# Another order of the head stages in the second super-block of a hybrid decoder step on one core

## The chip, the cores and the metric

One core of one Trainium2 chip runs the whole kernel. The metric is device time in microseconds: the median of the runs of one program on the chip. Lower is better.

## What the kernel computes

A prompt of 16 + 2048 tokens and 8 sample tokens pass through a trunk of two layers. Each layer projects the tokens (1024 wide) to 5120 channels, sends them through three groups of heads, gates each by SiLU, projects the 1536 mixed channels back and normalises. The core of the reference:

```python
u = jnp.einsum('btd,de->bte', x, w_in).astype(f32)
rg_c, rg_buf_new = _causal_conv(rg_in, rg_buf, rg_conv_w)
rg_h, h_new = _rglru(rg_c + rg_conv_b, h0, ...)                    # A: RG-LRU
y_rg = rg_h * jax.nn.silu(rg_z)
...
o, s_ret_new = _chunk_run(_ret_step, RET_CHUNK, s_ret, (q, k, v), lead)      # B: retention
...
o, s_gdn_new = _chunk_run(_gdn_step, GDN_CHUNK, s_gdn, (gq, gk, gv, g_log, beta), lead)   # C: gated DeltaNet
...
mix = jnp.concatenate([y_rg, y_ret, y_gdn], -1)
out = jnp.einsum('bte,ed->btd', mix, w_out.astype(f32))
y = _layernorm(DEEPNORM_ALPHA * x + out, ln_w, ln_b)
```

Inside a chunk of 64 tokens the gated DeltaNet solves a triangular system; the kernel inverts these triangles explicitly. The heads of one group don't depend on each other, nor the groups on one another, except that every DeltaNet head needs all key stages and the inverses.

## The kernel before

The tokens of a layer are taken in two super-blocks: columns 0 to 1023 (two blocks of 512), then 1024 to 2071 (three blocks of 384, 384 and 280, the samples among them). In each, the work is a row of sixteen **stages**, written out in the table `STAGES` (line 29): K0 to K3 make the DeltaNet keys, A0 to A3 are slabs of RG-LRU, B0 to B3 retention heads, C0 to C3 DeltaNet heads. A stage has slabs of 128 output channels: one for K, two for A (the convolution and the gate), four for B (q, k, v, gate), three for C. A slab is a projection `proj` (line 466 ff.): 24 matmuls for every token block, named `pj<-arena`, because float32 is computed as three products of two rounded halves; the weights are staged in `raw`, split on ScalarE and GpSimd and kept in `arena`. Two PSUM banks hold `pj`.

What a head does behind its projections (its recurrence and norm: `retention_bg`, `delta_bg`, `rglru_gates` and `rglru_scan`) is a generator that the `Pump` interleaves with the projections of the **next** stage. The triangular inverses (`inverses`, names `as_`, `tt`, `t`, `tn`, `prod`) are a second such stream. It begins behind the key stages, is spread over the slabs up to C0 (`n_inv` counts them) and is finished, in the order of writing, before C0.

`Recorder` notes all instructions in this order and then issues them in another: a list scheduler, driven by assumed costs, takes on every engine the earliest noted instruction that it expects to be ready (one that reads PSUM goes ahead on VectorE and ScalarE). So `STAGES` sets a priority, and the scheduler an order on every engine. On the chip each engine then keeps to that order.

Tiles share places, and a new tile waits for the last user of the old one. Those that matter here:

- `g` (the gate, two places): a stage's gate waits for the output of the stage two before it, to the end of the DMA `mix_d<-g` that stores it.
- `q` (two places): holds the q of a B or C stage; the inverses borrow one for their matrices `as_`. In the second super-block that place goes on to the q of C0.
- `a1` to `a4` (one place each): the working tiles of the generator that is running: `kv`, `sn` (B), `kk`, `uv`, `wq` (C), `r`, `ix`, `ch`, `cl`, then `s`, `y` (A). So the generators of successive stages follow each other.
- `kT` (two places): k of B, C and K, the convolution's result `c` of A; at the end of a layer two of the three places in which the weights of the output projection are staged (`raw<-in_wout`).

In the last stage of the second super-block (`end` in `rglru`) `c` lies in `tab`, and the gates' generator is started inside the stage. From there `wo_load` and `wo_free` bring the output weights in twelve pieces (`wh`, `wl` for the first two, `arena` for the others), as the projections' input is given up. Then the output projection runs over 17 row tiles (`pj` and `po`/`pd` of 512 columns).

```python
rows of the loop over stages (sblock):
n_inv = sum(len(SLABS[st[0]]) for st in STAGES[sb][4:STAGES[sb].index("C0")])
if i_st == 4:
    pump.drain()
    scales()
    pump.add_aux(inverses(), (78 if samp else 60) / (n_inv * nmm))
```

Of the kernel before, what the change touches and what calls it, by code (L numbers as in the profile page):

```python
# [25 lines left out]
SCK = 128.0 ** -0.5  # L26
HALF = 1024

STAGES = ("K0 K1 K2 K3 A0 B0 A1 C0 C1 B1 A2 C2 C3 B2 A3 B3".split(), "K0 K1 K2 K3 A0 B0 A1 C0 B1 C1 B2 C2 B3 C3 A2 A3".split())
NEG = -32768.0  # L30


# [306 lines left out]
def hymba_step(ctx: ExitStack, tc: tile.TileContext, x0t, x0, win, wab, wout, wg, vec, fbc, const, rope,  # L339
# [64 lines left out]
    def big(tag, name=None, n=1052, dt=F32, bufs=2):  # L404
        return wk.tile([128, n], dt, tag=tag, name=name or tag, bufs=bufs)
# [4 lines left out]
    def softplus(out, x, P, n, pre):  # L410
# [10 lines left out]
        for d in (15, 13, 11, 9, 7, 5, 3):  # L421
# [8 lines left out]
    SLABS = dict(K=(28,), A=(0, 4), B=(8, 12, 16, 20), C=(24, 32, 36))  # L430
    order = [(l, j + int(st[1])) for l in range(DEPTH) for sb in range(2) for st in STAGES[sb]
             for j in SLABS[st[0]]]
# [117 lines left out]
    def layer(l):  # L550
# [42 lines left out]
        def sblock(sb):  # L593
# [751 lines left out]
            def rglru(i):  # L1345
                end = samp and STAGES[1][-1] == f"A{i}"
                c = big("tab", "c", bufs=1) if end else big("kT", "c")
                conv(i, slab(), [VV("rgcw")[:, 4 * q + i:4 * q + i + 1] for q in range(4)], VV("rgcb")[:, i:i + 1], c)
                wgt = lay.tile([128, 2, 128], F32, name="wgt", tag="wgt", bufs=1)
                SP.dma_start(wgt, wg[l, :, i])  # L1350
                rx = []
                gates = rglru_gates(i, c, wgt, rx), 2 * len(blks) + 7
                if end:
                    pump.add(*gates)
                g = gate(slab())
                if not end:
                    pump_next(*gates)
                pump_next(rglru_scan(i, rx, g), 5)
# [75 lines left out]
            hook["last"] = last_slab  # L1434
            n_inv = sum(len(SLABS[st[0]]) for st in STAGES[sb][4:STAGES[sb].index("C0")])
            for i_st, st in enumerate(STAGES[sb]):
                if st == STAGES[1][-1] and samp:
                    wo_load(l)
# [193 lines left out]
    def wo_load(l):  # L1632
        raws, wo = [], {}
        wos["tiles"] = wo

        def stage(i):
            if i < 12:
                raws.append(big(("kT", "kT", "raw")[i % 3], "raw", n=1024, bufs=(2, 2, 1)[i % 3]))
                SP.dma_start(raws[i], wout[l, WO_ORDER[i]])

        def gen(lo, hi):
            for i in range(lo, hi):
                k = WO_ORDER[i]
                if k < 10:
                    wh, wl = arena[:, 2048 * k:2048 * k + 1024], arena[:, 2048 * k + 1024:2048 * k + 2048]
                else:
                    wh = wk.tile([128, 1024], F32R, tag=("q", "v")[k - 10], name="wh", bufs=2)
                    wl = wk.tile([128, 1024], F32R, tag=("q", "v")[k - 10], name="wl", bufs=2)
                A.copy(wh, raws[i])
                V.tensor_tensor(wl, raws[i], wh.bitcast(F32), op=OP.subtract)  # L1650
                wo[k] = (wh, wl)
                if i == 0:
                    stage(2)
                stage(i + 3)
                yield

        stage(0)
        stage(1)
        wos["gen"] = gen
        pump.add_aux(gen(0, 2), 2 / 60)  # L1660
# [129 lines left out]
```

## Time and profile before

| | us |
|---|---|
| median of 3 runs | 3231.73 (3229.43 to 3248.26) |
| profiled execution | 3247.79 |
| its span, first to last instruction | 3246.0 |
| TensorE busy in the span | 3143.9 |
| VectorE busy | 2040.6 |
| ScalarE busy | 1295.8 |
| GpSimd busy | 683.9 |

The profiled execution took 1.79 us more than its span. It lies near the slowest of the three runs, 16.1 us above their median. A layer takes about half of the span; in the first layer the second super-block runs from about 620 to 1285 us, in the second from about 2235 to 2912 us. PE stands for TensorE's matmuls, DVE for VectorE, ACT for ScalarE, POOL for GpSimd, SP for the queue that issues most DMAs. Every instruction goes through one helper, so all rows show its line 268; an instruction is told by the tile it writes and those it reads. "Idle before" and an engine and tile behind an arrow say how long the engine stood still and whose end it waited for. The granted clock of TensorE is 1.00 at 2.4 GHz and 0.50 at 1.2 GHz.

### The profile page before, as it was taken

The numbers are of one execution on the slowest core, as the hardware profiler recorded it, in microseconds if no ns is written. First come the engines' busy times: TensorE is split into PE (matmuls) and PEld (weight loads), VectorE is DVE, ScalarE is ACT, GpSimd is POOL, SyncE is SP. The second block draws the span as 40 slices with busy tenths as digits, with TensorE's granted clock in tenths as the row PEclk, the third lists the DMA queues.
The fourth block names the chain that finished last, engine by engine and source line by source line (L and its number), as shares of the span: only waits on it lengthen the run. The fifth ranks groups of instructions, "written<-read, shape, count | busy, mean of one in ns | idle before, by whom it ended". The sixth has DMA issues, their size and how long they took to land. (4 is left out here: it accounts for less than half of the span.)

```text
span 3246.0 us, 47389 instructions
## 1 busy us (share of the span) xinstructions
PE 3143.9 (97%) x18876; PEld 2758.9 (85%) x18876; DVE 2040.6 (63%) x3704; ACT 1295.8 (40%) x2732; POOL 683.9 (21%) x651
## 2 busy tenths in 40 slices
PE   8999999998999998999999999999989999998999
PEld 6888888898899998788778888888988999987886
DVE  6876565678745556656478756556876455566554
ACT  4454544543544445211243545444424444453110
POOL 2222221222312221111122222222222122121110
PEclk9999999998999999899999999999978999998999
DMA  4111211321111113555321111122201111135542
GB/s 151 61 67 46 67 49 56 104 82 40 49 46 56 41 51 123 168 167 161 112 95 54 61 47 67 43 67 103 73 33 43 51 58 41 51 108 179 156 143 70
DMA packets 137061, 262.97 MB, mean 81 GB/s; under 512 B 24368, under 2 KB 79600, under 8 KB 136840
## 3 DMA queue, kind: packets, MB, share of 16 engines
q1 hardware_dynamic: 113640, 179.91, 17.7%
q0 software_dynamic: 23200, 80.04, 6.8%
q8 instruction: 148, 2.42, 0.3%
q14 instruction: 73, 0.60, 0.1%
HBM read 195.13 MB, written 65.04 MB: 80 GB/s over the span
## 5 line engine op out<-in xcount | busy, mean ns | idle before, releaser
L268 PE MATMUL pj<-arena 128*128 128x512 f32 (+3 forms) x9760 | 2129.8, 362 | 39.3 <-DVE g L268 24.6
L268 PEld LDWEIGHTS pj<-arena 128*128 128x128 f32 (+1 forms) x9760 | 1637.4, 189 | 198.2 <-DVE g L268 26.5
L268 POOL TENSOR_TENSOR arena<-raw,arena 128x1024 fp32r<-128x1024 f32 x159 | 399.3, 2511 | 1205.2 <-ACT arena L268 1064.0
L268 ACT CAST arena<-raw 128x1024 fp32r<-128x1024 f32 x180 | 188.8, 1049 | 341.1 <-PE pj L268 183.0
L268 DVE SCALAR_TENSOR_TENSOR stg<-stg,eg,pd 128x128 f32<-128x128 f32 x264 | 90.9, 344 | 137.5 <-PE pd L268 135.7
L268 PE MATMUL pj<-arena,ah 128*128 128x512 f32 x512 | 164.8, 403 | 0.9 <-ACT ah L268 0.9
L268 ACT COPY ur<-pj 128x512 f32<-128x512 f32 (+2 forms) x160 | 80.3, 502 | 195.4 <-PE pj L268 194.9
L268 ACT ACT_TABLE_LOAD x106 | 136.0, 1283 | 26.5 <-DMA mix_d<-g 22.0
L268 ACT COPY sw<-pj 64x512 f32<-64x512 f32 (+2 forms) x160 | 80.0, 500 | 107.7 <-PE pj L268 60.4
L268 PEld LDWEIGHTS pj<-arena,ah 128*128 128x128 f32 x512 | 97.7, 192 | 23.8 <-ACT ah L268 1.0
L268 PE MATMUL pj<-arena,al 128*128 128x512 f32 (+1 forms) x296 | 112.3, 400 | 0.1
L268 PEld LDWEIGHTS pz<-stg,wq 128*128 128x128 f32 x512 | 90.2, 189 | 12.7 <-ACT wq L268 3.6
L268 DVE SCALAR_TENSOR_TENSOR g<-g,pj 128x512 f32<-128x512 f32 (+2 forms) x120 | 69.1, 579 | 50.1 <-ACT g L268 49.5
L268 PE MATMUL pz<-stg,wq 128*128 128x128 f32 x512 | 98.8, 274 | 1.6 <-ACT wq L268 1.4
L268 PE MATMUL pd<-kv 128*128 128x128 f32 x512 | 99.2, 276 | 0.0
L268 ACT CAST bh<-mb 128x512 fp32r<-128x512 f32 x32 | 19.8, 619 | 197.9 <-PE po L268 115.6
L268 DVE BATCH_NORM_STATS2 bs<-pz 128x6 f32<-128x128 f32 x128 | 37.9, 296 | 93.6 <-PE pz L268 93.5
L268 ACT ACTIVATE g<-pj 128x512 f32<-128x512 f32 (+2 forms) x120 | 61.5, 514 | 87.4 <-PE pj L268 85.5
L268 PEld LDWEIGHTS pd<-kv 128*128 128x128 f32 x512 | 86.8, 190 | 7.6
L268 PE MATMUL po<-arena,ah 128*128 128x512 f32 x288 | 92.9, 401 | 0.0
L268 ACT ACTIVATE wq<-pz,eg 64x128 f32<-64x128 f32 x128 | 43.0, 360 | 118.8 <-DVE kv L268 74.1
L268 DVE SCALAR_TENSOR_TENSOR qT<-ur,gcw,qT 128x1024 f32<-128x1024 f32 (+1 forms) x48 | 75.8, 1580 | 20.7 <-ACT qT L268 20.4
(388 smaller groups left out, 5166.7 us busy)
## 6 DMA issues: line engine op xcount, KB each, us to landing
raw<-in_win SPq DMA_DIRECT2D x160, 512.0 KB, 3.3
ma<-mix_d SPq DMA_DIRECT2D x31, 512.0 KB, 4.8
mix_d<-g POOLq DMA_DIRECT2D x24, 520.0 KB, 3.0
mix_d<-g POOLq DMA_DIRECT2D x24, 512.0 KB, 3.1
raw<-in_wout SPq DMA_DIRECT2D x24, 512.0 KB, 3.8
xr<-in_x SPq DMA_DIRECT2D x16, 512.0 KB, 4.0
x_d<-yo POOLq DMA_DIRECT2D x16, 512.0 KB, 3.3
sv<-row_d POOLq DMA_DIRECT2D x16, 512.0 KB, 4.4
```

What stands on the lines that cost most here:

```text
L268: return lambda *args, **kw: self._r.note(self._n, op, lambda: f(*args, **kw), args, kw)
```

## The change

One line changes: the sequence of stages of the second super-block, in both layers. The first super-block keeps its own.

```diff
-STAGES = ("K0 K1 K2 K3 A0 B0 A1 C0 C1 B1 A2 C2 C3 B2 A3 B3".split(), "K0 K1 K2 K3 A0 B0 A1 C0 B1 C1 B2 C2 B3 C3 A2 A3".split())
+STAGES = ("K0 K1 K2 K3 A0 B0 A1 C0 C1 B1 A2 C2 C3 B2 A3 B3".split(), "K0 K1 K2 K3 B0 A0 B1 C0 A1 C1 B2 C2 A2 C3 B3 A3".split())
```

The same sixteen stages run, A3 still last. Ahead of C0 there were A0, B0 and A1 with 8 slabs; now there are B0, A0 and B1 with 10, so `n_inv` is 10. Behind each stage its generator runs under another stage: C0 under A1 (before under B1), C2 under A2 (before under B3), C3 under B3 (before under A2), and under the last stage A3 that of B3 (before that of A2).

The instructions on each engine move with it. First VectorE in the second super-block of the first layer, where the scan of A0 ends (`s<-r,hcar,ix`, and `g<-s,g`, which gives A0's gate its output). Before:

```order
L268 SCALAR_TENSOR_TENSOR s<-r,hcar,ix 128x1040
L268 COPY hcar<-s 128x1
L268 TENSOR_TENSOR s<-r,h_121 128x8
L268 TENSOR_TENSOR s<-s,ix 128x8
L268 COPY h_121<-s 128x8
L268 SCALAR_TENSOR_TENSOR g<-s,g 128x1048
L268 SCALAR_TENSOR_TENSOR tt<-as__914,nbs,t_821 128x961
L268 TENSOR_REDUCE t_821<-tt 128x31
L268 STREAM_TRANSPOSE tt<-t_821 128x32x32
L268 SCALAR_TENSOR_TENSOR g<-g,pj 128x384 x2
```

The last row is A1's gate, four rows behind the scan; its tile is the place that A0's `g` gives up. Now, in the same place:

```order
L268 SCALAR_TENSOR_TENSOR s<-r,hcar,ix 128x1040
L268 COPY hcar<-s 128x1
L268 TENSOR_TENSOR s<-r,h_121 128x8
L268 TENSOR_TENSOR s<-s,ix 128x8
L268 COPY h_121<-s 128x8
L268 TENSOR_TENSOR sn<-qk,ct 128x512
L268 SCALAR_TENSOR_TENSOR g<-s,g 128x1048
L268 SCALAR_TENSOR_TENSOR prod<-as__915,nbt,gt 4x100
L268 TENSOR_REDUCE gt<-prod 4x10
L268 TENSOR_TENSOR sn<-qk,ct 128x512
L268 SCALAR_TENSOR_TENSOR prod<-as__915,nbt,gt 4x121
```

The large solve is over by then (only the samples' small one, `prod`, is left), the generator of B1 begins (`sn<-qk`), and the next gate in this place, that of C0, stands 52 rows behind `g<-s,g`.

Second, TensorE in the same super-block, where the third block of C0's first projection waits for the place of `as_`. Before, behind the recurrence of B0 (`pz`, `pd`), its norm (`pno`) and the first gates of A1 (`pgt`):

```order
L268 MATMUL po<-str_107,qT 16x128
L268 MATMUL pd<-tk 128x128
L268 MATMUL pno<-ct,sn 128x128 x8
L268 MATMUL pno<-ct,tk 128x16
L268 MATMUL pgt<-ch,wv 128x384 x2
L268 MATMUL pj<-arena 128x280 x24
```

Now it stands inside the recurrence of B1:

```order
L268 MATMUL po<-tk 16x128
L268 MATMUL pd<-kv 128x128
L268 MATMUL pz<-str_108,qT 128x128 x2
L268 MATMUL pd<-kv 128x128
L268 MATMUL pj<-arena 128x280 x24
```

From the transpose with which the inverses begin (`pn<-ct,nb`) to this row TensorE has 344 `pj` matmuls of 384 columns and 168 of 280 before; now 437 and 216, 29 in place of 16 `pz`, and 16 in place of 8 each of `qk`, `ptk` and `ptv`.

Third, VectorE at the end of the first layer's second super-block, ahead of the last gates' operand `cl`. Before:

```order
L268 TENSOR_TENSOR ix<-ix,s 128x1048
L268 SCALAR_TENSOR_TENSOR s<-r,hcar,ix 128x1040
L268 COPY hcar<-s 128x1
L268 TENSOR_TENSOR s<-r,h_121 128x8
L268 TENSOR_TENSOR s<-s,ix 128x8
L268 COPY h_121<-s 128x8
L268 SCALAR_TENSOR_TENSOR g<-s,g 128x1048
L268 TENSOR_TENSOR arena<-raw,arena 128x1024
L268 TENSOR_TENSOR cl<-c,ch 128x384 x2
```

Now:

```order
L268 TENSOR_SCALAR sn<-pz,mv,rs 128x128 x8
L268 TENSOR_SCALAR tk<-po,mv,rs 16x128
L268 SCALAR_TENSOR_TENSOR g<-g,pj 128x280
L268 SCALAR_TENSOR_TENSOR g<-sn,g 128x512
L268 TENSOR_TENSOR arena<-raw,arena 128x1024
L268 SCALAR_TENSOR_TENSOR g<-sn,g 128x512
L268 SCALAR_TENSOR_TENSOR g<-tk,g 128x16
L268 TENSOR_TENSOR cl<-c,ch 128x384 x2
```

Where the scan of A2 stood ahead of `cl`, the norm of retention head B3 stands now.

## Rows read from the trace of the kernel before

**Rows 1.** The page: busy time, share of the span, instructions of each engine.

```profile
PE 3143.9 (97%) x18876; PEld 2758.9 (85%) x18876; DVE 2040.6 (63%) x3704; ACT 1295.8 (40%) x2732; POOL 683.9 (21%) x651
```

**Rows 2.** Waits of TensorE, whole span: us in total, times, longest.

```profile
PE pj L268 <- DVE g L268: 24.6, 6, 10.7
PE pgt L268 <- ACT ch L268: 17.2, 2, 8.9
```

**Rows 3.** Windows: stretch, its length, busy time (instructions) of each engine, granted clock, DMA.

```profile
704.60:836.00 131.40, 114.92 (x890) 108.93 (x888) 108.84 (x189) 45.06 (x89) 28.46 (x21) 0.92 0.12 38
2317.90:2461.70 143.80, 126.65 (x888) 119.53 (x887) 109.67 (x189) 45.32 (x89) 28.75 (x20) 0.82 0.11 35
1262.00:1341.00 79.00, 61.83 (x296) 51.59 (x295) 58.73 (x87) 45.14 (x73) 10.77 (x16) 0.81 0.58 178
2890.00:2965.00 75.00, 59.52 (x286) 49.33 (x285) 57.94 (x86) 44.54 (x72) 11.26 (x13) 0.82 0.57 176
```

**Rows 4.** Windows again, those with a low granted clock.

```profile
785.00:801.00 16.00, 11.71 (x106) 10.94 (x107) 9.98 (x13) 4.55 (x9) 1.10 (x1) 0.51 0.07 26
830.00:840.00 10.00, 7.76 (x33) 5.86 (x34) 7.72 (x20) 3.49 (x7) 1.41 (x3) 0.66 0.19 66
1287.00:1313.00 26.00, 11.80 (x31) 8.27 (x31) 19.64 (x21) 18.18 (x22) 2.19 (x4) 0.54 0.52 172
...
2395.00:2443.00 48.00, 40.00 (x354) 36.37 (x355) 19.83 (x37) 9.80 (x21) 4.51 (x5) 0.50 0.06 23
...
2917.00:2943.00 26.00, 15.87 (x45) 11.61 (x46) 21.35 (x25) 19.84 (x24) 3.25 (x4) 0.54 0.64 212
```

**Rows 5.** Timeline, first layer, 782 to 836 us: start, us, engine, operation [idle before].

```profile
782.02 1.24 DVE L268 SCALAR_TENSOR_TENSOR g<-s,g 128x1048 f32<-128x1048 f32 x1
786.87 1.28 ACT L268 ACT_TABLE_LOAD   x1 [10.87 <-DMA mix_d<-g]
789.29 3.63 PE L268 MATMUL pj<-arena 128*128 128x280 f32 x14 [10.66 <-DVE g L268]
830.29 2.62 PE L268 MATMUL pno<-ct,sn 128*128 128x128 f32 x8 [2.95 <-DVE sn L268]
835.45 1.05 ACT L268 ACTIVATE qT<-pj,gcw 128x384 f32<-128x384 f32 x2 [0.48 <-DVE prod L268]
```

**Rows 6.** Groups of TensorE by form, 742.7 to 766.3 us: count | busy, mean ns.

```profile
L268 PE MATMUL pj<-arena 128*128 128x384 f32 x100 | 17.9, 335 | 0.0
L268 PE MATMUL pj<-arena 128*128 128x280 f32 x48 | 6.5, 291 | 0.0
```

**Rows 7.** Groups of VectorE by form, 704 to 836 us: count | busy, mean ns.

```profile
L268 DVE SCALAR_TENSOR_TENSOR c<-ur,vt,c 128x1040 f32<-128x1040 f32 x6 | 7.7, 1286 | 0.0
L268 DVE TENSOR_TENSOR sw<-sw,tabs 128x1048 f32<-128x1048 f32 x2 | 2.5, 1244 | 0.0
L268 DVE SCALAR_TENSOR_TENSOR tt<-as__914,nbs,t 128x625 f32<-128x625 f32 x1 | 1.4, 1387 | 0.0
```

**Rows 8.** Timeline of GpSimd and VectorE at 746 us.

```profile
746.08 2.26 POOL L268 TENSOR_TENSOR y<-r 128x1048 f32<-128x1048 f32 x1 [9.63 <-ACT r L268]
746.47 2.87 DVE L268 SCALAR_TENSOR_TENSOR tt<-as__914,nbs,t 128x529 f32<-128x529 f32 x1
```

**Rows 9.** Timeline, first layer's end of the second super-block, 1282 to 1316 us.

```profile
1282.21 3.12 PE L268 MATMUL pj<-arena 128*128 128x280 f32 x23
...
1290.48 0.79 PE L268 MATMUL pj<-wh,bh 128*128 128x512 f32 x1 [4.45 <-ACT wh L268]
...
1302.71 1.10 PE L268 MATMUL pgt<-ch,wv 128*128 128x384 f32 x2 [8.89 <-ACT ch L268]
```

**Rows 10.** DeltaNet head C3 in the first layer: its window, and its projections by form.

```profile
1214.90:1275.10 60.20, 60.20 (x420) 57.48 (x418) 34.65 (x77) 29.81 (x87) 11.68 (x13) 1.00 0.27 82
...
L268 PE MATMUL pj<-arena 128*128 128x384 f32 x168 | 37.4, 353 | 0.0
L268 PE MATMUL pj<-arena 128*128 128x280 f32 x72 | 12.7, 307 | 0.0
```

## The prediction, made before the changed kernel ran

> **What bounds the kernel now.** I read the page's engine table first: TensorE is busy for 3143.9 of 3246.0 us, no other engine for more than 63% [rows 1]. So the time is TensorE's work, its standstills (102 us) and whatever a low clock adds to its work. The change adds and removes no matmul; it can only move the second and third item. Then the list of TensorE's waits: two groups stand out, projections that wait for VectorE's `g` (24.6 us in six) and gates of RG-LRU that wait for ScalarE's `ch` (17.2 us in two) [rows 2]. The timeline puts both in the second super-block, one of each per layer, and nearly all that the change can touch lies around these four places. Their windows give the rest: how long the stretch is, how long TensorE is busy in it, and at which clock.
>
> The *start stretch* (the solve of the inverses until C0's q) lasts 131.4 us in the first layer and 143.8 us in the second, TensorE being busy for 114.92 and 126.65 [rows 3]. The same instructions run in both, so the 12 us between them are clock. In the first layer two pieces ran low: 11.71 x 0.49 + 7.76 x 0.34 = 8.3 us lost. In the second, 40.00 us of work ran at 0.50, that is 20 lost in that window alone [rows 4]. At full speed the work of this stretch is 114.9 - 8.3 = 106.6 us. Above that the first layer loses 24.8 us, the second 37.2.
>
> Why TensorE stands there: the timeline shows A0's scan end with `g<-s,g` at 782.02; that output is stored by a DMA, for which ScalarE stands 10.87 us before it may write A1's gate into the place, and TensorE 10.66 us because its PSUM bank isn't read [rows 5]. The scan itself is late since VectorE is in the solve. Later TensorE waits 2.95 us for B0's norm, and the q of C0 waits for the solve's `prod`, the last user of the place of `as_` [rows 5]. In both cases TensorE runs out of work it is allowed to do, while VectorE finishes a serial chain.
>
> The *end stretch* lasts 79 and 75 us, busy 61.83 and 59.52, idle 17.2 and 15.5 [rows 3]; low clock takes 11.80 x 0.46 = 5.4 and 15.87 x 0.46 = 7.3 more [rows 4]. Lost: 22.6 and 22.8. Here A3's gates wait 8.89 us for `ch`, whose place the scan of A2 still holds, and the output projection waits 4.45 us for the split of its second weight [rows 9].
>
> **The change part by part.** *Start.* TensorE now has work to do ahead of the release of `as_`: 93 more `pj` matmuls of 384 columns and 48 more of 280 (the counts in the section on the change). One of 384 costs 17.9 / 100 = 0.179 us, one of 280 6.5 / 48 = 0.135 us [rows 6]: 16.6 + 6.5 = 23.1 us. B1's recurrence moved ahead of that point adds 13 `pz`, 8 `qk` and 16 transposes with their partners; by the `pno` row, 2.62 / 8 = 0.33 us each [rows 5], at most 12 us for these 37; I take half, 6, since that row stands right behind a stall at low clock. Work ahead of the release: 106.6 + 29 = 135 us.
>
> VectorE's chain ahead of the same point grows too. B1 brings two rotations of at most three passes, 1.244 us each (the `sw` row), 7.5 us, and its head begins (a few `sn` and `kv`, taken as 4 us); A1's convolution, three passes of 1.286, goes [rows 7]. Net +8 us, bounds 0 (VectorE had 22.6 us of slack in 131.4 [rows 3]) and 12. So the release comes at 131.4 + 8 = 139.4 us or earlier, against 135 us of work: 0 to 4.4 us idle. I take 4 idle and 2 of low clock behind it, as the piece at 830 shows: 6 lost per layer. The gate's wait goes altogether: C0's `g` stands 52 VectorE rows behind the `g<-s,g` whose place it takes, where it was 4, and the two slabs between are 23 us against the 10.66 of that stall. Gain: 24.8 - 6 = 18.8 us in the first layer, 37.2 - 6 = 31.2 in the second.
>
> GpSimd splits the weights of two more slabs while the solve runs. A pass of the solve over 529 columns took 2.87 us where GpSimd had started a TENSOR_TENSOR 0.39 us before it [rows 8]; one over 625 columns took 1.39 [rows 7]. The Trainium skill, "SBUF — State Buffer", section "Who interferes with whom", says that a VectorE instruction with two SBUF inputs contends with a GpSimd instruction that reads SBUF, and that whoever comes second blocks until the first is done; the 2.87 us agree. By that rule each further split costs VectorE up to the difference, and the forecast would be some 6 us higher, 3181 by my estimate. In the sum itself this is inside the bound of 12 us above: two splits of 2.87 - 1.39 = 1.5 us are 3 us per layer.
>
> *End.* A2 now runs two stages earlier, so its scan no longer holds the place of A3's `ch` (VectorE's rows ahead of `cl` are now B3's norm), and `kT`, where the second output weight is staged, isn't A2's convolution any more. 8.89 + 4.45 = 13.3 of the 17.2 us go. What is late next: B3's norm, whose product TensorE awaits; the nearest row is the 2.95 us of B0's [rows 5]. Left: 17.2 - 13.3 + 3 = 7 idle and 4 of low clock, 11 per layer. Bounds: 3.9 (no new wait, full clock) and 22.6 (a wait as long as today's). I stay nearer to the lower since the new wait's row is short. Gain: 11.6 + 11.8 = 23.4 us.
>
> *Middle.* C1, C2 and C3 run under other stages (B2, A2, B3). The traced pattern is full: head C3 under A2 and what follows kept TensorE busy for all of 60.20 us at clock 1.00 [rows 10]. I count 0, because the order draws projections of later stages in between the heads' chains; bounds 0 and the third rival.
>
> Sum, against the profiled execution's 3247.8 us (its span and 1.8 around it): 3247.8 - 18.8 - 31.2 - 23.4 = 3174.4, say 3175. That execution is 16 us above the median of 3231.7; the 12 us of clock in the second layer's start stretch explain most of that, and they go with the stall. Against the median the change is -57 us, 1.75%.
>
> **The rivals.** *The start's stall only moves.* VectorE's chain is the bound of the solve; with 8 to 12 us more in it, and a head of its own started before the solve ends, the release of `as_` could come later by as much as TensorE got to do. For it: VectorE is busy for 108.84 of 131.4 us there. Against it: 10.66 of the 24.8 us is a gate waiting for a DMA, which vanishes with the place. Then half of the gain goes, with the low clock that follows a stall: 3175 + 25 = 3200 if half, and 3175 + 2 x 18.8 = 3213 if what is left is a stall of the first layer's size in both. I take 3213.
>
> *The end's gain doesn't come.* The output weights stream through a few staging places, the DMAs being 0.58 busy there [rows 3]; if their arrival sets the end, the waits for `wh` and `ch` are replaced by others of the same sum: 3175 + 23.4 = 3198, about 1% under the median.
>
> *Slower: DeltaNet heads starve under two-slab stages.* C3's head took 60.20 us with 168 projections of 384 and 72 of 280 [rows 10], 30.1 + 9.7 = 39.8 us by the prices above; the head's own matmuls are the other 20.4. Its length is a chain between engines, which the projections fill. C0 now runs under A1 and C2 under A2, two slabs each: 48 x 2 x 0.179 + 24 x 2 x 0.135 = 23.7 us. 20.4 + 23.7 = 44 of 60 us: 16 idle in each of four places, 64 in the two layers, plus low clock behind them as seen in the start stretches, 2 x 5.7 + 2 x 20 = 51. With the gains kept that is 3175 + 115 = 3290, 1.8% slower. It decides if the first projection of C1 (or C3) must wait for a place that the head before it holds to its end. For it: three heads share one set of working tiles. Against it: those are tiles of the generators, not of projections, and C3 itself, under the two slabs of A2, drew over three slabs' worth of projections and left nothing idle.
>
> *More than forecast.* If both new stalls are nil, 3175 - 2 x 6 - 2 x 7 = 3149, about 3150.
>
> **How the numbers follow.** About 1% (32 us) is what a measurement of this kernel can tell from no change. The forecast has 0.58; 3150 has 0.08; the start's stall moved (3213, within 1%) 0.14; the end's gain missing (3198, at the bound, half faster and half same) 0.12; starving heads 0.08. Faster: 0.58 + 0.08 + 0.06 = 0.72; same: 0.14 + 0.06 = 0.20; slower: 0.08. The forecast's own range: all of the unknown 12 us on VectorE and a tail at its upper bound in one layer make 3175 + 12 + 11.6 = 3199; 3156 is no idle time at the start and half at the end. For 8 in 10 I go to 3150 below and, to hold the moved stall and a little of the clock's scatter, 3225 above; the starving heads are left out.
>
> **What would show it.** Right: the list of TensorE's waits has no `pj` behind `g` of 10 us and no `pgt` behind `ch` of 8 us; the work from the solve's start to C0's q runs at clock 1.00 in both layers, without the 48 us at 0.50; a wait of a few us at most for C0's q; between the last projection and the gates at the end less than 8 us idle; TensorE's busy time falls by some 30 us, though no matmul went, since less of it runs at 0.50. Wrong: a new group of waits of `pj` behind `prod` or `qT` of 8 us or more (the moved stall); waits for `wh` or `arena` of more than 10 us per layer at the end; or idle time of TensorE under C0 and C2, with `pj` waiting for `q`, `kT` or `g` until the head's last instruction.

## The result, and the profile after

The changed kernel takes 3187.34 us (median of 4 runs, 3183.41 to 3194.39), the kernel before 3238.75 us (median of 4 runs, 3229.43 to 3248.26). The ratio is 0.9844, with a 95% interval of 0.9803 to 0.9884: 51 us or 1.6% faster. The forecast was 3175 us, 1.75% faster.

The profiled execution of the changed kernel took 3189.6 us, its span is 3187.8 us: 58.2 us less than before. First the page's engine rows; [rows 1] is their counterpart.

```profile
span 3187.8 us, 47369 instructions
PE 3128.2 (98%) x18876; PEld 2745.8 (86%) x18876; DVE 2050.1 (64%) x3704; ACT 1292.2 (41%) x2732; POOL 676.5 (21%) x651
```

TensorE is busy 15.7 us less with the same 18876 matmuls (less of its time at the low clock), and it stands still for 59.6 us in place of 102.1. The first five of its waits over the whole span (total, times, longest) show what went:

```profile
PE pj L268 <- ACT arena L268: 8.0, 3, 6.8
PE pj L268 <- ACT ah L268: 6.7, 2, 4.3
PE pno L268 <- DVE wq L268: 6.2, 4, 1.6
PE pz L268 <- DVE bs L268: 5.4, 12, 0.8
PE pj L268 <- DVE arena L268: 5.4, 5, 3.4
```

Both groups of [rows 2], the 24.6 us behind `g` and the 17.2 us behind `ch`, are gone, and none of their size stands in their place. The windows of the four places, the start stretch in both layers and then the end stretch in both (length, busy time of PE, PEld, DVE, ACT, POOL, granted clock, DMA), are to be held against [rows 3]. The start is cut again from the transpose that opens the solve to the q of C0; the end is cut a little differently, since other work stands there.

```profile
705.40:853.80 148.40, 145.53 (x1100) 139.91 (x1099) 116.31 (x201) 53.99 (x103) 31.22 (x27) 0.94 0.13 45
2299.60:2448.00 148.40, 145.52 (x1100) 139.89 (x1098) 116.31 (x201) 53.94 (x103) 31.06 (x26) 0.94 0.13 45
1254.00:1318.00 64.00, 54.22 (x261) 44.86 (x261) 48.94 (x83) 33.55 (x49) 7.57 (x13) 0.92 0.62 191
2850.00:2910.00 60.00, 53.18 (x244) 42.40 (x243) 47.47 (x80) 32.19 (x43) 7.11 (x10) 0.91 0.62 193
```

The start holds 1100 matmuls where it held 890. TensorE stands still for 2.9 us there where it stood still for 16.5 and 17.2. The clock is 0.94 in both layers, and that is now the larger loss: 145.5 x 0.06 = 8.7 us. At the end 9.8 and 6.8 us are idle (before 17.2 and 15.5), over windows that are 15 us shorter. The single events that stand for these numbers, from the timeline of TensorE, VectorE and ScalarE in the first layer:

```profile
792.98 2.02 DVE L268 SCALAR_TENSOR_TENSOR tt<-as__915,nbs,t 128x961 f32<-128x961 f32 x1
802.98 2.11 PE L268 MATMUL pg<-tn,ap 32*32 32x32 f32 x64 [1.30 <-DVE tn L268]
840.65 2.38 DVE L268 TENSOR_TENSOR_SCAN s<-r,hcar,ix 128x1040 f32<-128x1040 f32 x1
853.23 1.05 ACT L268 ACTIVATE qT<-pj,gcw 128x384 f32<-128x384 f32 x2 [0.93 <-DVE prod L268]
1274.31 0.23 PE L268 MATMUL pno<-ct,tk 16*128 16x16 f32 x1 [0.81 <-ACT sn L268]
1277.64 0.44 PE L268 MATMUL pgt<-ch,wv 128*128 128x384 f32 x1 [1.50 <-ACT wv L268]
1281.00 0.60 PE L268 MATMUL pgt<-ch,wv 128*128 128x280 f32 x1 [1.53 <-ACT r L268]
1314.64 1.22 PE L268 MATMUL pj<-arena,ah 128*128 128x512 f32 x2 [4.26 <-ACT ah L268]
```

The 10.66 us of [rows 5] have become 1.30 us, ahead of `pg`, the small matmuls with which the inverses are finished. A0's scan comes 38 us behind that wait; before, it came ahead of `pg` (and of the last pass of the solve, which is the first row here). B3's norm costs 0.81 us at the end, and the 8.89 us of [rows 9] are two waits of 1.5. The longest wait of the end is now 4.26 us (2.42 in the second layer) for `ah`, the tokens' operand of the output projection.

The low clock has moved. These windows are to be held against [rows 4]: in the start stretch of either layer, and one in the second layer's first super-block, whose sequence of stages did not change.

```profile
804.00:822.00 18.00, 18.00 (x204) 16.83 (x199) 4.77 (x7) 4.89 (x11) 2.73 (x3) 0.55 0.09 31
2399.00:2416.00 17.00, 17.00 (x174) 15.85 (x172) 4.00 (x6) 4.89 (x11) 2.73 (x3) 0.53 0.10 33
1786.00:1798.00 12.00, 12.00 (x102) 9.44 (x100) 5.53 (x6) 6.45 (x11) 0.00 (x0) 0.50 0.01 1
```

TensorE is busy all the time in each of them, and in each it runs the `pg` matmuls of 32x32 between its projections. The low pieces of the kernel before hold them too: the 48 us at 0.50 in [rows 4] begin with the stall for `g`, and the blocks of `pg` stand in them from 2406.57 to 2436.5 us.

A table of what was lost by stretch, worked out from windows of 4 us (standstill, and busy time times one minus the granted clock; us):

| stretch | before: idle, clock | after: idle, clock | gain |
|---|---|---|---|
| start, first layer | 16.5, 6.8 | 2.9, 8.5 | 11.9 |
| start, second layer | 17.1, 21.2 | 2.9, 8.6 | 26.8 |
| end, first layer | 17.2, 9.1 | 9.8, 4.5 | 12.0 |
| end, second layer | 15.5, 8.2 | 6.8, 4.6 | 12.3 |
| from the end of the first layer to the second start | 6.7, 1.7 | 6.8, 6.8 | -5.1 |

They sum to 57.9 of the 58.2 us by which the spans differ. The table compares two executions. That the gain of the start is 15 us larger in the second layer than in the first is the clock of the execution before, which ran the same work there at 0.82 and 0.92.

### The profile page after: what moved, and what is told of

It reads as the page before. It is cut to its first block, busy times and chain, and to the rows that moved or that the text cites. A ratio compares the mean times of both kernels' runs of the same rounds, so it can differ in the third digit from the quotient of the medians.

```text
span 3187.8 us, 47369 instructions
## 1 busy us (share of the span) xinstructions
PE 3128.2 (98%) x18876; PEld 2745.8 (86%) x18876; DVE 2050.1 (64%) x3704; ACT 1292.2 (41%) x2732; POOL 676.5 (21%) x651
## 5 line engine op out<-in xcount | busy, mean ns | idle before, releaser
L268 DVE SCALAR_TENSOR_TENSOR kT<-ur,gcw,kT 128x1024 f32<-128x1024 f32 (+1 forms) x48 | 69.4, 1446 | 21.9 <-ACT kT L268 21.4
```

What stands on the lines that cost most here:

```text
L268: return lambda *args, **kw: self._r.note(self._n, op, lambda: f(*args, **kw), args, kw)
```

## The experiments

All ratios are to the kernel before, with a 95% interval; the kernel before ran beside each group of four, 17 times, with medians of 3242.95 to 3244.39 us. Differences in us are between medians. Only the second super-block's sequence or what is named in the diff differs from the kernel named.

### The two halves of the change

Front alone:

```diff
-K0 K1 K2 K3 A0 B0 A1 C0 B1 C1 B2 C2 B3 C3 A2 A3
+K0 K1 K2 K3 B0 A0 B1 C0 A1 C1 B2 C2 B3 C3 A2 A3
```

> Only the front of the new sequence (B0 A0 B1 C0 A1 ..., the old end C3 A2 A3). Theory (the gains belong to two separate places): the wait of TensorE for g of 10.7 us and the half-speed piece behind it go, the wait for ch of 8 to 9 us at the end stays; 33 to 45 us under the kernel before, ratio about 0.988. Rival (the two places are one effect, a head chain that is late from the start to the end): the ch wait shrinks too and the time is 50 us or more under the kernel before, 0.984 or less. Rival (the front's stall only moves): under 10 us gained.

Measured: 3200.94 us, ratio 0.9868 (0.9842 to 0.9894), 43 us gained. The first of TensorE's waits is the old one at the end:

```profile
PE pgt L268 <- ACT ch L268: 17.9, 2, 9.5
```

End alone:

```diff
-K0 K1 K2 K3 A0 B0 A1 C0 B1 C1 B2 C2 B3 C3 A2 A3
+K0 K1 K2 K3 A0 B0 A1 C0 B1 C1 B2 C2 A2 C3 B3 A3
```

> Only the end of the new sequence (A0 B0 A1 C0 B1 C1 B2 C2 A2 C3 B3 A3). Theory: the wait for ch and that for wh go at both ends, the g wait of 10.7 us at the start stays; 18 to 24 us under the kernel before, ratio about 0.9935. Rival (C2 under the two slabs of A2 starves TensorE unless the front is changed too): waits of 5 us or more under A2 and no gain.

Measured: 3230.26 us, ratio 0.9957 (0.9938 to 0.9977), 14 us gained (7 to 20). Here the first wait is the one at the start:

```profile
PE pj L268 <- DVE g L268: 23.3, 4, 10.7
```

Each half removes its own wait and leaves the other as it was. 0.9868 x 0.9957 = 0.9826, the whole change 0.9844, within its interval: the two places are separate, as the first theory had it. The end's gain is below the 18 that were expected by the median, though its interval reaches 20.

### At the start: which stage is first, or how many slabs

The prediction had credited the start to 29 us more matmul work ahead of the release of `as_`. Two sequences part this from the order of A0 and B0. Both keep the new end and spread the inverses over 8 slabs. The first, against the run with the end alone:

```diff
-K0 K1 K2 K3 A0 B0 A1 C0 B1 C1 B2 C2 A2 C3 B3 A3
+K0 K1 K2 K3 B0 A0 A1 C0 B1 C1 B2 C2 A2 C3 B3 A3
```

> B0 A0 A1 C0 B1, then the new sequence: the old 8 slabs ahead of C0, but A0's place of g now goes to C0 and not to A1. n_inv = 8. Theory (the work that TensorE may do ahead of the release of the as_ place counts, the place of g is only where the shortage shows): the 10 us wait for g goes and a wait of 10 us or more shows elsewhere ahead of C0; within 12 us of the run with the new end alone. Rival (the place of g is the cause): no wait over 3 us there and 25 us or more under the run with the new end alone.

Measured: 3186.49 us, ratio 0.9823 (0.9801 to 0.9846): 44 us under the run with the new end alone, from exchanging A0 and B0 and nothing else. The theory falls in its size: it had allowed 12 us. The number of slabs is the old one and the time is that of the full change. The wait did move, as expected of it, to `pg`, but it is 4.50 us, not 10 or more (this view and the two like it below are cut a little behind the wait, so their counts are of a part of the block):

```profile
792.13 1.08 PE L268 MATMUL pg<-tn,ap 32*32 32x32 f32 x17 [4.50 <-ACT ttbd L268]
```

The rival isn't quite right either, since it allowed no wait over 3 us.

The second, against the changed kernel with `n_inv` = 8 (its own run is in the next part):

```diff
-K0 K1 K2 K3 B0 A0 B1 C0 A1 C1 B2 C2 A2 C3 B3 A3
+K0 K1 K2 K3 A0 B0 B1 C0 A1 C1 B2 C2 A2 C3 B3 A3
```

> A0 B0 B1 C0 A1, then the new sequence: 10 slabs ahead of C0, but A0's place of g goes to B1, whose gate comes two slabs later than A1's did. n_inv = 8. Theory (work ahead counts): within 12 us of the new sequence with n_inv = 8. Rival (the place of g is the cause): B1's gate waits for A0's output, 6 us or more per layer, 20 us or more slower than the new sequence with n_inv = 8.

Measured: 3250.9 us, ratio 1.002 (1.0006 to 1.0034). Ten slabs with A0 first gain nothing: 81 us slower than the same ten with B0 first (3170.21, below). Neither text named where it would wait. Not B1's gate but `pg` waits, for 20.70 us in the first layer and 21.5 in the second:

```profile
787.96 1.27 PE L268 MATMUL pg<-tn,ap 32*32 32x32 f32 x20 [20.70 <-DVE tn L268]
```

So the place of `g` isn't the cause. What the runs have in common is read from one window each, from the opening of the solve to the first `pg`: in order, the kernel before, A0 B0 B1, B0 A0 A1, and the changed kernel (columns as above; the third busy time is VectorE's).

```profile
704.60:792.90 88.30, 77.05 (x475) 76.10 (x474) 83.45 (x105) 31.27 (x60) 23.39 (x13) 0.95 0.13 43
```

```profile
705.50:788.00 82.50, 61.80 (x390) 61.41 (x388) 78.12 (x100) 26.87 (x50) 21.01 (x12) 0.90 0.12 39
```

```profile
705.10:792.10 87.00, 82.15 (x538) 80.00 (x536) 77.32 (x130) 29.32 (x63) 18.95 (x14) 0.99 0.13 45
```

```profile
705.40:803.00 97.60, 95.89 (x623) 93.39 (x621) 87.08 (x141) 35.14 (x71) 21.60 (x16) 1.00 0.13 46
```

With A0 first VectorE is busy for 95% of this window, and TensorE is busy for only 62 to 77 us ahead of `pg`. With B0 first VectorE is busy for 89% and TensorE for 82 to 96 us. The window is 82 to 88 us long in all but the last; what differs is how much of it TensorE fills. With A0 first its convolution, gates and scan stand among the passes of the solve:

```profile
771.50 3.38 DVE L268 SCALAR_TENSOR_TENSOR s<-y,s 128x1048 f32<-128x1048 f32 x1
...
777.78 1.24 DVE L268 TENSOR_TENSOR ix<-ix,s 128x1048 f32<-128x1048 f32 x1
779.06 2.38 DVE L268 TENSOR_TENSOR_SCAN s<-r,hcar,ix 128x1040 f32<-128x1040 f32 x1
...
782.02 1.24 DVE L268 SCALAR_TENSOR_TENSOR g<-s,g 128x1048 f32<-128x1048 f32 x1
783.17 1.85 DVE L268 SCALAR_TENSOR_TENSOR tt<-as__914,nbs,t 128x961 f32<-128x961 f32 x1
```

That is the kernel before: the last pass of the solve stands behind A0's scan. In the changed kernel the last pass is at 792.98 us and the scan at 840.65. In each pair that differs in the order of A0 and B0 alone, B0 first is faster, by 44 and by 81 us. That the place of the scan does it isn't shown, and one run speaks against it: with the old sequence at a pace of 6 slabs (next part) the scan too comes behind the last pass, and TensorE still waits 14.88 us:

```profile
785.57 1.85 DVE L268 SCALAR_TENSOR_TENSOR tt<-as__914,nbs,t 128x961 f32<-128x961 f32 x1
...
798.09 2.38 DVE L268 TENSOR_TENSOR_SCAN s<-r,hcar,ix 128x1040 f32<-128x1040 f32 x1
```

What the traces do show is that A0 first costs on one of two sides. At a pace of 8 with ten slabs the last pass comes equally early in both orders (76.1 us behind the opening of the solve with A0 first, 76.6 with B0 first), but A0 first leaves TensorE only 249 projections of 384 columns and 120 of 280 ahead of `pg`, where B0 first leaves 315 and 168; by the prices of [rows 6], 61 us against 79. At a pace of 6 TensorE has nearly the same projections in both orders (249 and 120, 246 and 120), but the last pass comes 71.7 us behind the opening with A0 first and 63.0 with B0 first. Why the fixed order leaves TensorE less to do ahead of `pg` when A0 is first isn't separated by any run; the scheduler sets that order by its assumed costs.

### The pace at which the inverses are noted

```diff
-n_inv = sum(len(SLABS[st[0]]) for st in STAGES[sb][4:STAGES[sb].index("C0")])
+n_inv = 8
```

> The new sequence, but the inverses spread over 8 slabs instead of 10. Theory (what counts is the projection work that may run ahead of the solve's end, and the places of g): within 8 us of the changed kernel, C0's q free some us earlier. Rival (the slower spreading by n_inv = 10 is what left VectorE free for A0's scan): the scan and g late again, a wait of 5 to 10 us per layer, 15 to 30 us slower than the changed kernel.

Measured: 3170.21 us, ratio 0.9779 (0.9751 to 0.9807), beyond what either text expected: 17 us under the changed kernel's 3187. Its start stretch:

```profile
704.30:853.30 149.00, 148.28 (x1166) 144.72 (x1165) 122.43 (x215) 58.69 (x113) 35.64 (x28) 0.99 0.15 48
2287.00:2436.00 149.00, 148.25 (x1166) 144.56 (x1164) 122.37 (x215) 58.56 (x113) 35.44 (x27) 0.99 0.14 48
```

Idle 0.7 us and clock 0.99, 2.4 us lost per layer (from windows of 4 us) where the changed kernel loses 11.4. Most of what is gained is low clock (8.5 us against 1.7), the rest idle time. The changed kernel's own `n_inv` of 10 puts the last pass 11 us later (87.6 us behind the opening of the solve against 76.6). This run also says what the slabs are worth: at the same pace of 8, with B0 first, ten slabs are 16 us under eight (3186.49 us, above), though the intervals of the two just touch. So the two more slabs do count; the pace of 10 that comes with them in the changed kernel costs about as much again. Two more values:

```diff
-n_inv = sum(len(SLABS[st[0]]) for st in STAGES[sb][4:STAGES[sb].index("C0")])
+n_inv = 8 + sb
```

> The new sequence, n_inv = 9 in the second super-block. Theory (8 to 10 differ by a small wait for tn and the low clock behind it): between the runs with 8 and 10, no wait for tn or one under 1 us if it is as good as 8. Rival (8 is a lucky case of where the small matmuls fall): 9 is no better than 10.

Measured: 3183.32 us, ratio 0.9817 (0.9793 to 0.9842). The wait ahead of `pg` is 0.50 us, so there is none to speak of, and yet the clock falls behind it (0.57 over the 23 us from there on):

```profile
798.60:822.00 23.40, 23.32 (x299) 22.11 (x300) 10.51 (x12) 7.12 (x15) 3.93 (x6) 0.57 0.01 1
```

The run lies between those with 8 and 10, as the theory had it, but no better than 10 by the intervals, which is the rival's outcome; that 8 is a lucky case stays open. A short wait alone doesn't account for the low clock: it is 0.50 us here and 0.33 with 8, and the piece at 1786 us of the changed kernel had none.

```diff
-n_inv = sum(len(SLABS[st[0]]) for st in STAGES[sb][4:STAGES[sb].index("C0")])
+n_inv = 8 - 2 * sb
```

> The new sequence, n_inv = 6 in the second super-block. Theory (VectorE does the solve at its own pace from n_inv = 8 down): within 8 us of the run with n_inv = 8, so 10 to 25 us under the changed kernel. Rival (a solve that is noted too early holds up A0's convolution and scan and with them g): 10 us or more slower than the run with n_inv = 8, with waits for g or c of several us.

Measured: 3206.01 us, ratio 0.9888 (0.9862 to 0.9914), the rival's size, 36 us slower than 8. But not by its mechanism: nothing waits for `g` or `c`; TensorE reaches `pg` too early and waits 4.92 us for the solve, whose last transpose `tn` ends 0.1 us before the row, and the clock is 0.50 from there on for 20 us:

```profile
773.62 3.40 PE L268 MATMUL pg<-tn,ap 32*32 32x32 f32 x64 [4.92 <-issue]
```

The same line put into the kernel before, with its old sequence:

> The old sequence, the inverses noted at a rate for 6 slabs instead of 8 in the second super-block. Theory (the wait for g comes from the places and from the scan of A0 behind the solve, which the sequence decides): the wait of about 10 us stays, within 10 us of the kernel before. Rival (the pace at which the solve is noted is all that the new sequence changed for the better): the wait goes and 25 us or more are gained.

Measured: 3236.73 us, ratio 0.9976 (0.9956 to 0.9995). The wait for `g` went and one of 14.88 us for the solve stands in its place, as the row shows. It is a mixed answer to the texts: the wait named by the theory is gone, and its time isn't.

```profile
791.92 1.30 PE L268 MATMUL pg<-tn,ap 32*32 32x32 f32 x21 [14.88 <-ACT ttbd L268]
```

Pace alone, with the old sequence, doesn't do it. The stall at the start takes the name of whatever stands next on TensorE when its work runs out.

More work than ten slabs, also with `n_inv` = 8:

```diff
-K0 K1 K2 K3 B0 A0 B1 C0 A1 C1 B2 C2 A2 C3 B3 A3
+K0 K1 K2 K3 B0 A0 B1 A1 C0 C1 B2 C2 A2 C3 B3 A3
```

> B0 A0 B1 A1 C0 C1 B2 C2 A2 C3 B3 A3 with n_inv = 8: 12 slabs ahead of C0, and C0's head under C1. Theory (once the work ahead covers the solve, more of it gives nothing): within 8 us of the new sequence with n_inv = 8. Rival of the prediction (heads under other stages starve TensorE): waits of 5 us or more under C1 or B2 and 15 us or more slower; rival (the release still bounds): 5 us or more faster.

Measured: 3176.93 us, ratio 0.9796 (0.9774 to 0.9818), within 8 us of the ten slabs at the same pace. Ten cover the solve.

### The low clock beside the small matmuls

The first attempt let the scheduler put another ready matmul behind every four of the 32x32 matmuls (eight rows of the trace, in which each of these float32 matmuls stands as two), in both super-blocks:

```diff
+                while run >= 4 and self.ops[i].small and here[e]:
+                    aside.append((self.ops[i].first, i))
+                    i = heapq.heappop(here[e])[1]
...
+                run = run + 1 if self.ops[i].small else 0
```

> The new sequence, and the scheduler puts another ready matmul behind every four of the 32x32 matmuls of the inverses. Theory (the clock falls behind the blocks of 64 and 32 small matmuls): the pieces at clock 0.50 at 805 to 822 and 2400 to 2416 us go, 8 to 9 us each, and so does the one at 1786 to 1798; 15 to 22 us under the changed kernel. Rival (the clock falls because of the 1.3 us wait for tn ahead of them, or on its own): the same low pieces at the same places, within 5 us of the changed kernel.

Measured: 3267.17 us, ratio 1.0074 (1.005 to 1.0099), 80 us slower than the changed kernel. The theory falls, with its sign. Windows from the first layer's first super-block, where the changed kernel runs the same small matmuls in blocks:

```profile
196.00:216.00 20.00, 20.00 (x147) 13.19 (x146) 12.05 (x13) 7.10 (x10) 3.73 (x3) 0.71 0.23 79
216.00:236.00 20.00, 20.00 (x144) 13.01 (x143) 5.71 (x6) 4.26 (x10) 0.00 (x0) 0.61 0.01 2
```

```profile
200.00:215.00 15.00, 15.00 (x285) 12.65 (x284) 10.73 (x13) 9.07 (x16) 0.57 (x1) 1.00 0.12 45
```

The first two are the mixed kernel, at 0.71 and 0.61; the last is the changed kernel, at 1.00. Spread out, the small matmuls take 40 us (199 to 239 us) in place of some 12, and the clock is low for most of it.

So the next theory was that a short stage costs less. It was tried by noting both halves of them together, in both super-blocks:

```diff
                 for q in range(2):
...
-                    yield
                     pg = pt("pg").rearrange("p (s c) -> p s c", c=32)
...
-                    yield
```

> The new sequence with n_inv = 10, but both halves of the 32x32 matmuls of the inverses noted together (no other work noted between them). Theory formed after the four-and-one mixture failed (the clock is low for as long as the stage of small matmuls lasts, so a short stage costs less): the stage shrinks from 23 to 10 to 14 us, the low piece from 17 us to 4 to 6, 10 to 16 us under the changed kernel, near the run with n_inv = 8. Rival (n_inv = 8 was faster because the solve ended earlier on VectorE): within 5 us of the changed kernel.

Measured: 3185.91 us, ratio 0.9822 (0.9796 to 0.9848), no difference from the changed kernel that the intervals show. It tells nothing of the theory: the stage still took 22 us, at 0.53; its groups still stand apart, with projections between them while VectorE and ScalarE turn round their results.

```profile
804.00:826.00 22.00, 21.77 (x288) 20.34 (x289) 5.90 (x8) 4.76 (x12) 2.77 (x4) 0.53 0.08 25
```

The same edit, with `n_inv = 8 - 2 * sb` besides:

> The new sequence, n_inv = 6 in the second super-block, and both halves of the small matmuls noted together. Theory (short stage of small matmuls, little time at low clock): up to 8 us under the run with n_inv = 6 alone, low pieces of at most 4 us at the start stretch of both layers. Rival (density makes it worse): a longer low piece behind the denser stage, 5 us or more slower.

Measured: 3207.78 us, ratio 0.9892 (0.9867 to 0.9916), the same as with `n_inv` = 6 alone. The stage was shorter (16.3 us in place of 20) and the clock stayed at 0.50 throughout, so the expected 4 us were not seen:

```profile
774.70:791.00 16.30, 13.81 (x260) 13.26 (x260) 7.82 (x16) 2.83 (x7) 0.43 (x1) 0.50 0.01 2
```

In the run with `n_inv` = 8 the same stage, with TensorE busy for 15.89 of 16 us, ran at 0.89:

```profile
794.00:810.00 16.00, 15.89 (x290) 15.05 (x291) 9.60 (x13) 4.21 (x11) 2.46 (x4) 0.89 0.13 43
```

What decides between 0.5 and 0.9 there isn't settled by these runs. They show that the low clock comes in the stage of small matmuls, that there it comes without a wait too, and that spreading them made it longer. They also show that part of it is scatter between executions. Eleven of the kernels here have the same first super-block. Over 24 us from 2 us ahead of its first `pg`, TensorE was busy for 24.00 us in both layers of all eleven, and the clock was 1.00 in eleven of these 22 stretches, 0.93 in three and 0.72 to 0.79 in eight. Two of them, the second layer of the kernel before and of the run with the end alone:

```profile
1800.13:1824.13 24.00, 24.00 (x327) 19.89 (x325) 17.07 (x17) 15.43 (x24) 3.77 (x3) 1.00 0.22 73
1801.83:1825.83 24.00, 24.00 (x302) 19.66 (x300) 13.47 (x15) 11.56 (x19) 2.00 (x2) 0.72 0.12 45
```

In the start stretch it looks less like scatter. Over the 24 us from the first `pg` the clock was 0.93 in all four stretches of the two runs with B0 A0 B1 and `n_inv` = 8, and 0.52 to 0.72 in all eight of the four runs with B0 A0 B1 and 9 or 10.

## Why the prediction was right, and where it was off

**What bounds the kernel.** Right: TensorE stands still 42.5 us less and is busy 15.7 us less, and that is the whole gain. The four places were the ones.

**The start.** The work of the stretch was put at 135 us; measured 145.5 - 8.7 = 137. The idle time was put at 4 us per layer; measured 2.9. What failed in size is the term "2 of low clock behind it": it was 8.5 and 8.6. The forecast took low clock to follow a stall and so to shrink with it; it came in the stage of the small matmuls, with 1.3 us of waiting ahead of it. With it the gains of 18.8 and 31.2 us came out as 11.9 and 26.8, 11.3 us short. Another 5.1 us went the same way in the second layer's first super-block, which the change doesn't touch; with the scatter found there that is bad luck, and the fast run with `n_inv` = 8 had the same. Together they are about the 15 us by which the profiled execution missed the forecast (3189.6 against 3174.4).

The reason given for the start was half right. "TensorE runs out of work it is allowed to do, while VectorE finishes a serial chain" holds. "VectorE had 22.6 us of slack in 131.4" was read from a window too long: up to the end of the solve VectorE was busy for 83.45 of 88.30 us, and the slack lay behind. The extra 29 us of work were not what decided: the old 8 slabs with B0 first, and the new end, come to the same time as the change (0.9823 and 0.9844), and 10 slabs with A0 first to that of the kernel before (1.002). The decisive part is one that the prediction did not price by itself, B0 ahead of A0 (44 us at 8 slabs). The slabs do add to it, 16 us at the same pace, which the slower pace of 10 gives back. So the size of the start's gain came out near the forecast partly by luck. The wait for the place of `g` was where the shortage showed, since with another sequence or pace it stood at `pg` with 14.88 or 20.70 us.

The rise of VectorE's chain was put at 8 us (bounds 0 and 12). The q of C0 came 147.9 us behind the opening of the solve in either layer, against 130.9 us before: a rise of 17 us, beyond the bounds. TensorE had work until then, so it cost little: ScalarE waited 0.93 us for `prod`, and TensorE was idle for 2.9 us in the whole stretch.

On GpSimd's two extra splits: from the opening of the solve to its last pass GpSimd begins six splits before and seven after, one more and not two, and the 31 passes of the solve took 34.0 us before and 31.9 after (VectorE's group of `tt<-as_` from 704 to 803 us). What the prediction read from one pass holds: in the changed kernel, where no GpSimd tensor instruction stands beside it, the pass of 529 columns took 1.19 us in place of 2.87. The rule of the Trainium skill, "SBUF — State Buffer", section "Who interferes with whom", agrees with this pair. But the total fell, since A0's `y<-r` is gone from the stretch and the splits meet other passes. The 3 us that the estimate added per layer weren't seen.

**The end.** Right: 11 us of loss per layer were forecast, 14.3 and 11.4 measured; gains of 11.6 and 11.8, measured 12.0 and 12.3. The wait for B3's norm was put at 3 us and is 0.8; in its place stands the wait for `ah`, 4.26 and 2.42 us, which the forecast didn't name. So the idle time of 7 us, measured 9.8 and 6.8, came out about right from another wait. The timing of the end alone, 14 us (7 to 20), is below the 23.4 of the sum; its profiled execution still has the stall at the start, whose loss in the first layer (31.3 us) was 8 us above that of the kernel before.

**The middle.** Right with 0. The two middles (first and second layer) show the starving rival wrong, at clock 1.00 with 2.5 us idle in 400:

```profile
853.80:1254.00 400.20, 397.67 (x2695) 382.77 (x2696) 240.44 (x486) 196.82 (x493) 102.00 (x108) 1.00 0.16 56
2448.00:2850.00 402.00, 399.42 (x2719) 384.51 (x2720) 241.86 (x490) 198.43 (x499) 99.96 (x101) 1.00 0.17 57
```

**The signs.** Two of the signs named in advance didn't come. The start stretch ran at 0.94 and not at 1.00, and TensorE's busy time fell by 15.7 us and not by some 30. Both come from the low clock.

**The other rivals.** "The start's stall only moves" is wrong for this change, but right for neighbours of it: it moved to `pg` with the old sequence at a pace of 6 slabs and with A0 first among ten slabs. "The end's gain doesn't come" is wrong. "More than forecast", about 3150, would have needed both new stalls nil and the clock full; the run with `n_inv` = 8 has the first at the start and came to 3170.21, the fastest of all. It beats both kernels.

## What to carry to other kernels

Where the busiest engine stalls, take the window that ends at the stall, not at the end of the stage, and look at the engine that it waits for there: here it was 95% busy, and 83% of the longer window looked like slack. Which stage stands first beside a long serial chain on a second engine can matter more than how much work stands beside it: here the order was worth 44 us and two more slabs 16. The name of the tile in a wait says what stood next in the order, not what was short: try a second sequence before giving that tile another place.

## What was not expected of the hardware

The granted clock fell to 0.50 with TensorE busy without a gap: 12.00 of 12.00 us in 1786 to 1798 us, ahead of which it ran blocks of 32x32 matmuls (from 1779.07 us) and waited for nothing. The same blocks ran at 1.00 in the first layer of the same execution (200 to 215 us). Over 22 such stretches of the same instructions the clock was 1.00 in half and lower in half. One other matmul behind every four of them came with a longer low piece: 20 us each at 0.71 and 0.61 where the blocks had 1.00. A low clock in a profile is therefore no proof of a stall ahead of it.
